# One layer of a hybrid decoder: lo parts of weights and diagonals of norms move from GpSimd to VectorE

## The chip, the cores and the metric

The kernel runs on one core of a Trainium2 chip. The metric is the device time of one execution in microseconds (us); the median of several runs counts. The engines are TensorE (PE in the profile, its weight loads PEld), VectorE (DVE), ScalarE (ACT), GpSimd (POOL) and SyncE (SP), which only issues transfers here.

## What is computed

The reference is one decoder layer on x of 512 rows and 1024 columns, in float32:

```python
h = rms_norm(x, attn_pre_g)
q_a, k_a, v_a, q_b, k_b, v_b = split(h @ w_in)
y_a = rms_norm(sliding_window_attention(q_a, k_a, v_a, sinks, alibi), swa_out_g)
y_b = rms_norm(softmax(q_b0 k_b0) v_b - lam * softmax(q_b1 k_b1) v_b, subln_g) * 0.8
x = x + rms_norm(concat(y_a, y_b) @ w_out, attn_post_g)
u = causal_dwconv3(rms_norm(x, ffn_pre_g) @ w_up)
x = x + rms_norm((gelu(u_g) * u_v) @ w_down, ffn_post_g)
```

`y_a` has 8 query heads over 2 key heads and a window of 128; `y_b` has 4 heads, each with two score maps of 64 columns and values of 128.

## The kernel before, in words

**Hi and lo parts.** Each matrix product runs in a reduced float32 format (F32R), with both operands split into a hi part (the value rounded to the format) and a lo part (the rest). A product is three matmuls: hi x hi, hi x lo, lo x hi. `load_split` (line 108) brings a weight of 128 x 1024 (or 128 x 960) in from memory over SP's queue (line 118), lets ScalarE copy it to hi (line 119), and lets VectorE or GpSimd subtract to give lo (line 120). Which of the two it is, the argument `slow` says. `raw` has two buffers for what comes in, and the pool of hi and lo tiles has three of each.

**The order of weights.** `Stream` (line 123) holds a list of loads and keeps two ahead of the one in use. The list (lines 153 to 161) has 29 loads: 6 for values, 10 for queries and keys, 13 for the output projection (8, then 5 once more). All are marked slow, and then `W_FIRST = 10` and `W_LAST = 10` take the mark off the first ten and the last ten. So nine splits run on GpSimd: those of the last six loads of queries and keys, and of the first three of the output projection. Later weights (up and down projection) always take VectorE.

**Norms.** `spread_a` (line 167) turns a row of sums of squares into a factor that is the same in all partitions. TensorE sums over partitions (line 174), VectorE adds epsilon (177 or 179), GpSimd takes the power -1/2 (181), VectorE splits the result into hi and lo columns (184, 185), and `eng` multiplies the identity by each column (190). The results are two diagonals of 128 x 128 for each block of 128 rows, up to 128 x 512 in one instruction. `spread_b` (196) multiplies them by ones on TensorE (200) and copies the result out on ScalarE (202). The call for the first norm (244) passes VectorE as `eng`; the six others (one at 619, five at 478) use the default, GpSimd: four of them make diagonals of 128 x 512, two of 128 x 256.

**The stages.** First the transposed x and the first keys and queries are handled (216 to 242). Then the sliding-window attention and the differential attention run as chains of small steps (`swa_a` to `swa_e`, `diff_a` to `diff_e`). Between these steps a queue of filler work for TensorE is drained: projections (356), values (276), the output projection (516). Each filler has a cost in us, and `fill(us)` (260) takes as many as the chain step leaves room for. After that come the row norms (642, 664), the up projection with convolution (698, 808), and the down projection with seven products in place of eight (885). The framework lays the instructions of each engine out in a fixed order when the kernel is built; an engine runs them in that order, and each waits for its inputs.

**Names and lines in the steps.** A finished projection is multiplied out of its bank by VectorE (351, `evac`). Keys are split by ScalarE (389) and VectorE (390) and copied to the other half of the partitions by transfers that GpSimd issues (391, 392). Queries are scaled and split by ScalarE (381) and VectorE (382); TensorE needs both for the scores (397, 398). VectorE takes the scores out with their minimum (425), ScalarE exponentiates (430), VectorE combines the two maps (434 to 436), TensorE transposes (452) and VectorE splits the transposed block (402). The window's output is scaled at 626, each head's at 484. GpSimd also fills masks (321 to 334), sums squares of x (239), and makes the row norms' roots (637 to 639).

Of the kernel before, what the change touches and what calls it, by code (L numbers as in the profile page):

```python
# [13 lines left out]
ALU = mybir.AluOpType  # L14
# [4 lines left out]
D = 1024  # L19
NT = S // P  # L20
NK = D // P
# [14 lines left out]
PAD = 72  # L36

WARM = 8

W_FIRST, W_LAST = 10, 10  # L40

V_AFTER = 1

# [16 lines left out]
def fl(t):  # L60
    return t.bitcast(F32)
# [16 lines left out]
def hymba_layer(ctx, tc, x, st, wv, wqk, w_out, w_up, w_down, conv, cols, lam_in, sinks, gpost, gffn, gfin, out):  # L78
    nc = tc.nc
    TT = nc.vector.tensor_tensor  # L80
# [24 lines left out]
    a8 = Arena(wk, T8, [P, NT, S], F32R, "a8")  # L105


    def load_split(src, slow=False, p=None, big=False, r=None):
        n = src.shape[-1]
        if r is None:  # L110
            r = raw.tile([P, n], F32, tag="raw", name="wr")
        if big:
            t = a8.get()
            h, l = (t[:, 2 * m:2 * m + 2].rearrange("p a s -> p (a s)") for m in range(2))
        else:
            t = None
            h, l = ((p or wsp).tile([P, n], F32R, tag=m, name=f"w{m}") for m in ("hi", "lo"))
        nc.sync.dma_start(r, src)
        ACT(h, r, AF.Copy)  # L119
        (nc.gpsimd if slow else nc.vector).tensor_tensor(l, r, fl(h), op=ALU.subtract)  # L120
        return (h, l, t) if big else (h, l)

    class Stream:
# [5 lines left out]
        def next(self):  # L129
            while len(self.made) < min(self.used + 1 + self.ahead, len(self.jobs)):  # L130
                src, kw = self.jobs[len(self.made)]
                self.made.append(load_split(src, **kw))
            self.used += 1
            return self.made[self.used - 1]
# [15 lines left out]
    ident = const.tile([P, P], F32, name="ident")  # L150
    make_identity(nc, ident)

    slow = dict(slow=True)
    jobs = []
    q = [(wqk[i], slow) for i in range(10)]
    o = [(w_out[k], slow) for k in range(NK)]
    v = [(wv[i], slow) for i in range(6)]
    nv = 2 + 2 * V_AFTER
    jobs += v[0:3] + q[0:nv] + v[3:6] + q[nv:10] + o + [(w, dict(big=True, **kw)) for w, kw in o[4::-1]]
    for n in [*range(W_FIRST), *range(len(jobs) - W_LAST, len(jobs))]:  # L160
        jobs[n] = jobs[n][0], {**jobs[n][1], "slow": False}
    W = Stream(jobs, 2)

    ones_r = const.tile([P, P], F32R, name="ones_r")
    nc.vector.tensor_copy(ones_r, ones)

    def spread_a(sq, ts_, n=None, eps=None, r=None, eng=nc.gpsimd):


        if r is None:  # L170
            r = small.tile([P, NT], F32, tag="rb", name="rb")
        o = banks.get()
        for t in ts_:
            nc.tensor.matmul(o[:, t:t + 1], lhsT=sq[:, t * P:(t + 1) * P], rhs=ones[:, 0:1], start=True, stop=True)
        c, cs = slice(ts_[0], ts_[-1] + 1), slice(ts_[0] * P, (ts_[-1] + 1) * P)
        if eps is None:
            nc.vector.tensor_scalar(r[:, c], o[:, c], 1.0 / n, EPS, op0=ALU.mult, op1=ALU.add)
        else:
            TT(r[:, c], o[:, c], eps[:, c], op=ALU.add)
        banks.free(o)  # L180
        nc.gpsimd.tensor_tensor(r[:, c], r[:, c], mhalf[:, c], op=ALU.pow)
        rh = small.tile([P, NT], F32R, tag="rh", name="rh")
        rl = small.tile([P, NT], F32, tag="rl", name="rl")
        nc.vector.tensor_copy(rh[:, c], r[:, c])
        TT(rl[:, c], r[:, c], fl(rh[:, c]), op=ALU.subtract)
        ds = []
        for part in (fl(rh), rl):
            d = t2()
            shape = [P, len(ts_), P]
            eng.tensor_tensor(  # L190
                d[:, cs].rearrange("p (t q) -> p t q", q=P), ident.unsqueeze(1).broadcast_to(shape),
                part[:, c].unsqueeze(2).broadcast_to(shape), op=ALU.mult)
            ds.append(d)
        return ds, cs

    def spread_b(ds, cs):

        o, rb = banks.get(), f2.get()
        for m, d in enumerate(ds):
            nc.tensor.matmul(o[:, cs], lhsT=ones_r, rhs=d[:, cs], start=(m == 0), stop=(m == 1))  # L200
        a2.free(*ds)
        ACT(rb[:, cs], o[:, cs], AF.Copy)
        banks.free(o)
        return rb
# [10 lines left out]
    xss = f2.get()  # L215
    for k in range(NK):
        r = a4.get()
# [8 lines left out]
        h, l = t2(), t2()  # L226
# [14 lines left out]
        a4.free(r)  # L241
        a2.free(h, l)
    rs1 = const.tile([P, NT], F32, name="rs1")
    rbc = spread_b(*spread_a(xss, range(NT), D, r=rs1, eng=nc.vector))
    f2.free(xss)


# [228 lines left out]
    def diff_d(h, ts_):  # L476
        pv, sq = soft[h]
        soft[h] = pv, sq, spread_a(sq, ts_, eps=zq[h])
# [139 lines left out]
    def swa_d():  # L618
        soft["a"] = spread_a(sqa[0], range(NT), 4 * P)
        f2.free(sqa[0])  # L620
# [14 lines left out]
    def sum_rstd(s2):  # L635

        nc.gpsimd.tensor_scalar(s2[:, 0:1], s2[:, 0:1], 1.0 / D, EPS, op0=ALU.mult, op1=ALU.add)  # L637
        nc.gpsimd.tensor_scalar(s2[:, 1:2], s2[:, 1:2], 1.0 / D, s2[:, 0:1], op0=ALU.mult, op1=ALU.add)
        nc.gpsimd.tensor_tensor(s2[:, 1:2], s2[:, 1:2], mhalf[:, 0:1], op=ALU.pow)  # L639
        return s2[:, 1:2]  # L640
# [54 lines left out]
    def early_weights(c):  # L695
        ew.append(load_split(w_up[order[c]], big=True)[0:2])
# [49 lines left out]
    for h, last in enumerate((3, 7, 11, 13)):  # L746
        n, ts_ = last + DEP + 1, range(NT) if h < 3 else range(2, 4)
# [4 lines left out]
    for n in range(2, len(steps) + DEP):  # L752
        if n < len(steps):
            h, i = steps[n]
# [80 lines left out]
    for n, f in enumerate(order):  # L835
# [4 lines left out]
        else:  # L840
            w = U.next()
# [3 lines left out]
        if n % 2:  # L845
            k = n // 2
# [42 lines left out]
    def prepare():  # L889
        p, q = steps_d[len(ready)]  # L890
        kind, src = products[p]
        src = w_down[q, src] if isinstance(src, int) else sums[src, q]

        n = len(ready)
        r = None if n % 3 == 0 else wsum.tile([P, D], F32, tag=f"b{n % 6 - n % 6 // 3 - 1}", name="wr")
        w = load_split(src, r=r, p=dw if n % 4 == 3 else None)
        a = rows(q, kind)
        ah = sp.tile([P, 2, S // 2], F32R, tag="ah", name="ah")
        al = sp.tile([P, 2, S // 2], F32R, tag="al", name="al")
        split(a, ah, al)  # L900
        ready.append((*w, ah, al))
# [93 lines left out]
    for s in two:  # L995
# [4 lines left out]
        r = sum_rstd(s2[s])  # L1000
# [59 lines left out]
```

## Time and profile before

| | before |
|---|---|
| median of 3 runs | 742.37 us (739.88 to 742.78) |
| the profiled execution: time | 741.13 us |
| its span, first to last instruction | 739.4 us |
| mean granted TensorE clock | 0.991 |
| TensorE busy | 717.2 us, 97% |
| VectorE busy | 557.2 us, 75% |
| ScalarE busy | 377.5 us, 51% |
| GpSimd busy | 108.8 us, 15% |

The busy shares are means over all stages. An engine's idle time counts only where another waits for it, and a row of the timeline ends with the idle time before it in brackets and what ended it. The granted clock is given as a share of 2.4 GHz: 1.00 is 2.4 GHz, 0.50 is 1.2 GHz. Letters before the colon of a tile name are the program's names; `a` is a tile of the attention's arenas, `bank` a PSUM bank.

### The profile page before, as it was taken

To read this page: it belongs to the slowest core of one execution; us is meant where nothing else is said; L and a number is where in the kernel's file an instruction comes from. 1 tells how busy PE (TensorE), PEld (TensorE's weight loads), DVE (VectorE), ACT (ScalarE), POOL (GpSimd) and SP (SyncE) were. 2 spreads that over 40 slices of the span, in tenths; PEclk is the share of its full clock that TensorE was granted. 3 is DMA by queue.
4 is the path that set the end of the run, shared out by engine and by line. 5 is a ranking of instruction groups with operands and counts; after the bars stand their busy time and mean duration, and the time that the engine had idled before them with its cause. 6 is when DMAs were issued, how large, how long until landed. Compare 5 with 4: busy or idle time off the path is not lost.

```text
span 739.4 us, 9503 instructions
## 1 busy us (share of the span) xinstructions
PE 717.2 (97%) x3416; PEld 599.3 (81%) x3416; DVE 557.2 (75%) x868; ACT 377.5 (51%) x652; POOL 108.8 (15%) x154
## 2 busy tenths in 40 slices
PE   8999998988999999999999999999999999999995
PEld 6787897767789988888888888888888888888884
DVE  7899968988779478685675757657566699988983
ACT  5288865756466334433434334333333666656661
POOL 6300145451333010000000000000000000000301
PEclk9999998999999999999999999999999999999999
DMA  7432314235455476555565555655576555556631
GB/s 226 148 101 69 88 59 114 57 86 170 116 170 172 171 257 241 186 204 195 170 207 190 203 185 198 204 181 200 175 252 215 160 193 199 199 187 189 205 131 58
DMA packets 36815, 124.43 MB, mean 168 GB/s; under 512 B 4512, under 2 KB 5152, under 8 KB 36768
## 3 DMA queue, kind: packets, MB, share of 16 engines
q1 hardware_dynamic: 30240, 103.38, 43.3%
q0 software_dynamic: 6528, 20.45, 7.8%
q8 instruction: 27, 0.44, 0.3%
q14 instruction: 20, 0.16, 0.1%
HBM read 102.31 MB, written 18.87 MB: 164 GB/s over the span
## 4 chain that ended last, share of the span: by engine, by line
PE 68%; DVE 0%; POOL 0%; ACT 0%; issue 0%; POOLq 0%; DVEq 0%; ACTq 0%
PE bank L703 16%; PE bank L702 16%; PE bank L704 16%; PE bank L907 7%; PE bank L909 7%; PE bank L908 7%; PE bank L668 0%; DVE f L1003 0%; POOL r L637 0%; DVE f L661 0%; DVE a L656 0%; ACT f L657 0%; ACT jk L944 0%; POOLq L1056 0%; POOL r L639 0%
## 5 line engine op out<-in xcount | busy, mean ns | idle before, releaser
L120 DVE TENSOR_TENSOR wlo<-wr,whi 128x1024 fp32r<-128x1024 f32 (+1 forms) x132 | 161.0, 1220 | 114.4 <-ACT whi L119 114.2
L119 ACT ACTIVATE whi<-wr 128x1024 fp32r<-128x1024 f32 (+1 forms) x141 | 149.0, 1057 | 166.1 <-PE bank L703 103.7
L702 PE MATMUL bank<-hTh,whi 128*128 128x512 f32 (+1 forms) x496 | 191.3, 386 | 0.0
L703 PE MATMUL bank<-hTl,whi 128*128 128x512 f32 (+1 forms) x496 | 191.3, 386 | 0.0
L704 PE MATMUL bank<-hTh,wlo 128*128 128x512 f32 (+1 forms) x496 | 191.2, 386 | 0.0
L702 PEld LDWEIGHTS bank<-hTh,whi 128*128 128x128 f32 x496 | 93.2, 188 | 18.8
L704 PEld LDWEIGHTS bank<-hTh,wlo 128*128 128x128 f32 x496 | 93.2, 188 | 18.6
L703 PEld LDWEIGHTS bank<-hTl,whi 128*128 128x128 f32 x496 | 93.2, 188 | 18.6
L908 PE MATMUL bank<-whi,al 128*128 128x512 f32 x224 | 87.1, 389 | 0.0
L909 PE MATMUL bank<-wlo,ah 128*128 128x512 f32 x224 | 87.1, 389 | 0.0
L907 PE MATMUL bank<-whi,ah 128*128 128x512 f32 x224 | 87.1, 389 | 0.0
L848 ACT ACTIVATE a<-ct 128x512 f32<-128x512 f32 x32 | 20.2, 631 | 90.3 <-DVE ct L813 90.3
L811 ACT ACTIVATE ct<-bank,conv_sb 128x512 f32<-128x512 f32 x64 | 48.6, 760 | 9.3 <-PE bank L704 9.3
L812 DVE SCALAR_TENSOR_TENSOR ct<-bank,conv_sb,ct 128x511 f32<-128x511 f32 x64 | 47.6, 744 | 7.7 <-ACT ct L811 7.7
L907 PEld LDWEIGHTS bank<-whi,ah 128*128 128x128 f32 x224 | 42.0, 188 | 8.9 <-ACT m L957 0.2
L909 PEld LDWEIGHTS bank<-wlo,ah 128*128 128x128 f32 x224 | 42.0, 188 | 8.8
L908 PEld LDWEIGHTS bank<-whi,al 128*128 128x128 f32 x224 | 42.0, 188 | 8.7
L813 DVE SCALAR_TENSOR_TENSOR ct<-bank,conv_sb,ct 128x510 f32<-128x510 f32 x64 | 47.7, 746 | 1.3
L827 DVE TENSOR_TENSOR b<-b,b 128x1024 f32<-128x1024 f32 x32 | 38.9, 1216 | 7.2 <-DMA b<-in_w_down 7.2
L402 DVE TENSOR_TENSOR al<-act,ah 128x512 fp32r<-128x512 f32 x48 | 32.8, 684 | 2.1 <-ACT ah L401 2.1
L401 ACT ACTIVATE ah<-act 128x512 fp32r<-128x512 f32 x48 | 29.5, 615 | 8.4 <-DVE act L849 5.6
L366 PE MATMUL bank<-hTh,whi 128*128 128x512 f32 x80 | 32.9, 411 | 0.0
(203 smaller groups left out, 1145.1 us busy)
## 6 DMA issues: line engine op xcount, KB each, us to landing
wr<-in_w_up SPq DMA_DIRECT2D x64, 512.0 KB, 3.6
b<-in_w_down SPq DMA_DIRECT2D x32, 512.0 KB, 4.5
wr<-in_w_down SPq DMA_DIRECT2D x24, 512.0 KB, 3.7
wr<-in_w_out SPq DMA_DIRECT2D x13, 512.0 KB, 4.3
wr<-in_wqk SPq DMA_DIRECT2D x10, 512.0 KB, 3.6
U<-b POOLq DMA_DIRECT2D x8, 512.0 KB, 3.7
W<-b POOLq DMA_DIRECT2D x8, 512.0 KB, 3.0
V<-b POOLq DMA_DIRECT2D x8, 512.0 KB, 3.0
```

Of the source, the lines that this page charges most:

```text
L119: ACT(h, r, AF.Copy)
L120: (nc.gpsimd if slow else nc.vector).tensor_tensor(l, r, fl(h), op=ALU.subtract)
L702: nc.tensor.matmul(u[:, c0:c1], lhsT=h[:, c], rhs=hTh[k][:, c0:c1], start=(k == 0), stop=False)
L703: nc.tensor.matmul(u[:, c0:c1], lhsT=h[:, c], rhs=hTl[k][:, c0:c1], start=False, stop=False)
L704: nc.tensor.matmul(u[:, c0:c1], lhsT=l[:, c], rhs=hTh[k][:, c0:c1], start=False, stop=(k == NK - 1))
L811: ACT(ct, u, AF.Identity, bias=w(3), scale=w(2))
L812: STT(ct[:, 1:S], u[:, 0:S - 1], w(1), ct[:, 1:S], ALU.mult, ALU.add)
L813: STT(ct[:, 2:S], u[:, 0:S - 2], w(0), ct[:, 2:S], ALU.mult, ALU.add)
L827: TT(rawb[a], rawb[a], rawb[b], op=ALU.add)
L907: nc.tensor.matmul(o, lhsT=ah[:, j, rs], rhs=wh[:, cs], start=first and j == 0, stop=False, skip_group_check=True)
L908: nc.tensor.matmul(o, lhsT=al[:, j, rs], rhs=wh[:, cs], start=False, stop=False, skip_group_check=True)
L909: nc.tensor.matmul(o, lhsT=ah[:, j, rs], rhs=wl[:, cs], start=False, stop=last and j == 1, skip_group_check=True)
```

## The change

All lo parts of weights are made by VectorE, and all diagonals of norms too. The lists of loads and their order, the calls of `spread_a` and the power at line 181 are as they were. GpSimd keeps that power, the masks, its transfers, the sums at line 239 and the row roots.

```diff
--- before.py
+++ after.py
@@ -37,8 +37,6 @@
 
 WARM = 8
 
-W_FIRST, W_LAST = 10, 10
-
 V_AFTER = 1
 
 NORM_ACT = 2
@@ -105,7 +103,7 @@
     a8 = Arena(wk, T8, [P, NT, S], F32R, "a8")
 
 
-    def load_split(src, slow=False, p=None, big=False, r=None):
+    def load_split(src, p=None, big=False, r=None):
         n = src.shape[-1]
         if r is None:
             r = raw.tile([P, n], F32, tag="raw", name="wr")
@@ -117,7 +115,7 @@
             h, l = ((p or wsp).tile([P, n], F32R, tag=m, name=f"w{m}") for m in ("hi", "lo"))
         nc.sync.dma_start(r, src)
         ACT(h, r, AF.Copy)
-        (nc.gpsimd if slow else nc.vector).tensor_tensor(l, r, fl(h), op=ALU.subtract)
+        TT(l, r, fl(h), op=ALU.subtract)
         return (h, l, t) if big else (h, l)
 
     class Stream:
@@ -150,21 +148,18 @@
     ident = const.tile([P, P], F32, name="ident")
     make_identity(nc, ident)
 
-    slow = dict(slow=True)
     jobs = []
-    q = [(wqk[i], slow) for i in range(10)]
-    o = [(w_out[k], slow) for k in range(NK)]
-    v = [(wv[i], slow) for i in range(6)]
+    q = [(wqk[i], {}) for i in range(10)]
+    o = [(w_out[k], {}) for k in range(NK)]
+    v = [(wv[i], {}) for i in range(6)]
     nv = 2 + 2 * V_AFTER
-    jobs += v[0:3] + q[0:nv] + v[3:6] + q[nv:10] + o + [(w, dict(big=True, **kw)) for w, kw in o[4::-1]]
-    for n in [*range(W_FIRST), *range(len(jobs) - W_LAST, len(jobs))]:
-        jobs[n] = jobs[n][0], {**jobs[n][1], "slow": False}
+    jobs += v[0:3] + q[0:nv] + v[3:6] + q[nv:10] + o + [(w, dict(big=True)) for w, kw in o[4::-1]]
     W = Stream(jobs, 2)
 
     ones_r = const.tile([P, P], F32R, name="ones_r")
     nc.vector.tensor_copy(ones_r, ones)
 
-    def spread_a(sq, ts_, n=None, eps=None, r=None, eng=nc.gpsimd):
+    def spread_a(sq, ts_, n=None, eps=None, r=None):
 
 
         if r is None:
@@ -187,7 +182,7 @@
         for part in (fl(rh), rl):
             d = t2()
             shape = [P, len(ts_), P]
-            eng.tensor_tensor(
+            TT(
                 d[:, cs].rearrange("p (t q) -> p t q", q=P), ident.unsqueeze(1).broadcast_to(shape),
                 part[:, c].unsqueeze(2).broadcast_to(shape), op=ALU.mult)
             ds.append(d)
@@ -241,7 +236,7 @@
         a4.free(r)
         a2.free(h, l)
     rs1 = const.tile([P, NT], F32, name="rs1")
-    rbc = spread_b(*spread_a(xss, range(NT), D, r=rs1, eng=nc.vector))
+    rbc = spread_b(*spread_a(xss, range(NT), D, r=rs1))
     f2.free(xss)
```

## Rows read from the trace of the kernel before

**Rows 1.** Stretches: us, busy by engine (instructions), PEclk, DMA share, GB/s.

```profile
100.00:110.00 10.00, 10.00 (x53) 8.81 (x53) 4.57 (x14) 6.50 (x12) 7.10 (x5) 1.00 0.34 106
110.00:175.00 65.00, 56.90 (x268) 45.65 (x268) 57.81 (x126) 40.60 (x97) 32.32 (x33) 0.95 0.34 88
175.00:205.00 30.00, 29.12 (x155) 24.07 (x155) 21.25 (x51) 16.87 (x39) 8.15 (x11) 1.00 0.54 164
```

**Rows 2.** Timeline of TensorE: start, us, what, idle before with its releaser.

```profile
122.04 0.48 PE L397 MATMUL bank<-a,a 128*128 128x256 f32 x1 [1.96 <-DVE a L382]
...
143.98 0.50 PE L200 MATMUL bank<-a,ones_r 128*128 128x512 f32 x1 [0.60 <-POOL a L190]
145.12 0.50 PE L200 MATMUL bank<-a,ones_r 128*128 128x512 f32 x1 [0.64 <-POOL a L190]
...
150.37 0.39 PE L397 MATMUL bank<-a,a 128*128 128x256 f32 x1 [2.02 <-DVE a L382]
...
170.31 0.44 PE L397 MATMUL bank<-a,a 128*128 128x384 f32 x1 [1.84 <-DVE a L382]
```

**Rows 3.** Single microseconds after the first of these waits, columns as before.

```profile
122.00:123.00 1.00, 0.96 (x4) 0.86 (x5) 0.96 (x2) 0.00 (x0) 0.00 (x0) 0.58 0.58 111
128.00:129.00 1.00, 1.00 (x4) 0.62 (x3) 0.96 (x3) 0.09 (x1) 0.90 (x2) 0.50 0.00 0
```

**Rows 4.** Timeline of GpSimd: three of the six splits from 110 to 175.

```profile
115.79 2.43 POOL L120 TENSOR_TENSOR wlo<-wr,whi 128x1024 fp32r<-128x1024 f32 x1
118.58 2.85 POOL L120 TENSOR_TENSOR wlo<-wr,whi 128x1024 fp32r<-128x1024 f32 x1 [0.36 <-ACT whi L119]
...
166.89 2.81 POOL L120 TENSOR_TENSOR wlo<-wr,whi 128x1024 fp32r<-128x1024 f32 x1
```

**Rows 5.** Timeline of VectorE.

```profile
119.24 3.45 DVE L382 SCALAR_TENSOR_TENSOR a<-f,a 64x512 fp32r<-64x512 f32 x2
...
129.85 0.48 DVE L436 SCALAR_TENSOR_TENSOR a<-a,zd 128x256 f32<-128x256 f32 x1
...
146.08 0.68 DVE L382 SCALAR_TENSOR_TENSOR a<-f,a 64x512 fp32r<-64x512 f32 x1
...
147.58 2.73 DVE L382 SCALAR_TENSOR_TENSOR a<-f,a 64x512 fp32r<-64x512 f32 x1
...
164.84 0.16 DVE L185 TENSOR_TENSOR rl<-rb,rh 128x4 f32<-128x4 f32 x1
...
167.51 3.46 DVE L382 SCALAR_TENSOR_TENSOR a<-f,a 64x512 fp32r<-64x512 f32 x2
...
171.82 1.22 DVE L120 TENSOR_TENSOR wlo<-wr,whi 128x1024 fp32r<-128x1024 f32 x1
172.95 0.75 DVE L484 SCALAR_TENSOR_TENSOR f<-bank,g_sub,f 128x512 f32<-128x512 f32 x1
```

**Rows 6.** Line 190, the diagonals: duration min/median/max in ns, first and last start.

```profile
L190 POOL TENSOR_TENSOR a<-ident,rh x6: 612/1040/1041, 127.1 to 203.4; 128x512 fp32r<-128x512 f32 x4, 128x256 fp32r<-128x256 f32 x2
...
L190 DVE TENSOR_TENSOR a<-ident,rh x1: 683/683/683, 31.3 to 31.3; 128x512 fp32r<-128x512 f32 x1
```

**Rows 7.** Groups of VectorE by form, 100 to 205 us: busy, mean ns, idle before.

```profile
L382 DVE SCALAR_TENSOR_TENSOR a<-f,a 64x512 fp32r<-64x512 f32 x6 | 10.3, 1712 | 0.2
...
L626 DVE SCALAR_TENSOR_TENSOR a<-a,cols_sb,f 128x512 f32<-128x512 f32 x4 | 4.6, 1188 | 0.0
...
L436 DVE SCALAR_TENSOR_TENSOR a<-a,zd 128x256 f32<-128x256 f32 x4 | 3.8, 945 | 0.1
...
L185 DVE TENSOR_TENSOR rl<-rb,rh 128x4 f32<-128x4 f32 x4 | 2.2, 561 | 0.0
```

**Rows 8.** Groups of GpSimd: the splits.

```profile
L120 POOL TENSOR_TENSOR wlo<-wr,whi 128x1024 fp32r<-128x1024 f32 x9 | 22.7, 2527 | 19.0 <-ACT whi L119 18.9
```

**Rows 9.** Line 120 up to 100 us: what VectorE waited for before its splits.

```profile
  ACT whi L119: 2.0, 3
```

**Rows 10.** A stretch with two splits on VectorE, columns as in rows 1.

```profile
45.00:50.00 5.00, 4.98 (x30) 4.24 (x30) 4.91 (x15) 5.00 (x14) 0.00 (x0) 1.00 0.36 107
```

## The prediction

> **What bounds the kernel now.** I read the stretches first, then TensorE's idle time in them, then what ended each wait. Nine lo splits and six pairs of diagonals are all that moves, and they lie between 100 and 205 us; so that stretch is cut in three [rows 1]. Outside it the change touches no instruction. From 100 to 110 TensorE is never idle and VectorE is busy for 4.57 of 10 us. From 110 to 175 TensorE is busy for 56.90 of 65 us at a granted clock of 0.95, and VectorE for 57.81: it is the fuller engine here. From 175 to 205 TensorE loses under 1 us. What can be won or lost is therefore in the middle 65 us: 8.1 us of idle TensorE, and 5% of clock.
>
> The larger waits of that idle time are five [rows 2]. Three are for L382 (the lo rows of a query) and last 1.96, 2.02 and 1.84 us; two, 0.60 and 0.64 us, are for the diagonals that GpSimd makes at L190. Right after the first the granted clock is low: 0.58 in the microsecond from 122, 0.50 in the one from 128 [rows 3], 1.2 instead of 2.4 GHz. About 7 us at half clock lose some 3.4 us, and 5% of 65 us is 3.3: so this is the one such stretch in the 65 us, and the waits of 2.02 and 1.84 us were followed by none.
>
> Why is L382 late? Six splits run on GpSimd in the 65 us; the first, second and last start at 115.79, 118.58 and 166.89 [rows 4]. The second ends at 121.43. VectorE's pair of L382 starts at 119.24 and takes 3.45 us, where one of them alone takes 0.68 [rows 5]: it ends 1.26 us after GpSimd's split. The pair at 167.51 takes 3.46 and ends 1.27 us after the last split. So an instruction of VectorE with two inputs in SBUF stands still while GpSimd's tensor_tensor runs. It is no share of bandwidth, since the rest of each pair takes its usual time.
>
> **The change, part by part.** *Added to VectorE:* a split of 128x1024 takes 1.22 us, and the next instruction starts 1.13 us after it [rows 5]; nine are 10.2. A full diagonal takes 0.68 us there, against 1.04 on GpSimd [rows 6]; the twelve are eight full ones and four of half width (0.4 each, an estimate from the ratio of GpSimd's two, 0.61 to 1.04): 5.4 + 1.6 = 7.0. Together 17.2 us. Inside the 65 us it is six splits and three pairs of full diagonals: 6.8 + 4.1 = 10.9.
>
> *Taken from VectorE:* the blocked time. By groups from 100 to 205 [rows 7]: L382 10.3 less 6 x 0.68 = 6.2; L626 4.6 less 4 x 0.75 (the 0.75 is L484's, of the same size [rows 5]) = 1.6; L436 of 256 columns 3.8 less 4 x 0.48 = 1.9; L185 2.2 less 4 x 0.16 = 1.6. That is 11.3 us, a floor, since L436's other lengths are left out. L382, L626 and by their starts half of the other two lie inside the 65 us: 6.2 + 1.6 + 1.8 = 9.6. So VectorE's load there goes from 57.8 to 57.8 - 9.6 + 10.9 = 59.1 us, hardly more, though it does 10.9 us more work.
>
> *Taken from GpSimd:* 22.7 us of splits [rows 8] and all diagonals. Nobody waits for those splits (each is needed two weights later), so this gains nothing itself. Its copies of keys (L391, L392) are queued behind splits and come earlier; I put that at nothing, because no TensorE wait of rows 2 is for them. It keeps the power at L181, the masks, the sums at L239 and the row roots of L637 to L639. The hop from VectorE to GpSimd and back for the power stays. The raw buffers come free 1.3 us sooner per split (2.5 against 1.22); the next loads start earlier on SP's queue, whose order does not change, and a later stage with those loads on time gains nothing.
>
> *A new wait:* a split at the head of VectorE's queue waits for its hi copy on ScalarE. Queued behind it are the evictions of scores (L425) and the next L382, for which TensorE waits. The ten splits that VectorE makes before 100 us cost 2.0 us of such waiting in 3 cases [rows 9]: between 0 and 0.67 us each. I take 0, since the order is laid out by readiness (at 119.24 both L382 were ahead of any other work), and keep 0.67 for the range.
>
> *The first three splits* (100 to 110 and at the edge) are hidden by VectorE's 5.4 idle us there; without that cover they would cost 3.4 us.
>
> Now wait by wait. **First (1.96):** two splits (2.26) come ahead of the pair, whose block (3.45 - 1.36 = 2.09) goes: +0.2 if both are ahead, -0.9 if the second falls behind the pair; I take -0.4. **The half clock** after it: 0 to -3.4. A wait cut from 2.0 to 1.6 need not end it, but two waits of this length left the clock at full, so I take it as gone; VectorE, with a pair of diagonals more there, cannot follow all of it: -2.5. **The diagonals (0.60 + 0.64):** each is 0.36 shorter on VectorE, -0.7 if nothing goes between, 0 if something does; -0.4. **Second L382 (2.02):** its block (2.73 - 0.68 = 2.05) goes, a pair of diagonals (1.36) comes ahead: -0.7 with the split behind, +0.4 with it ahead; -0.6, since the split started on GpSimd when this L382 was next. **Third (1.84):** block 3.46 - 1.36 = 2.1 against the same 1.36 and 1.13: -0.7 to +0.4; -0.5. After 175: nothing, because VectorE is idle for 9 of 30 us there.
>
> Sum: -0.4 - 2.5 - 0.4 - 0.6 - 0.5 = -4.4 us. Ends: +1.0 (all splits ahead, the clock unchanged) and -6.4. A check by load: VectorE can be 98% busy with TensorE full, as from 45 to 50 us, with splits of its own among its work (4.91 and 4.98 of 5) [rows 10]. 59.1 / 0.98 = 60.3 us, so the 65 us cannot shrink by more than 4.7, and the sum just fits under that.
>
> The profiled execution took 741.13 us (span 739.40 and 1.73 around it), 1.24 under the median of the three runs, 742.37; on it the sum gives 736.7, on the median 738.0, which I forecast.
>
> One rule speaks against the change. The trace shows VectorE at 89% of the 65 us, the fuller engine [rows 1]. The Trainium skill (Perfetto Trace Analysis, Optimizing Scalar/DVE Operations) says that work may be offloaded from a saturated VectorE, even to GpSimd, and adds that the two share a read port, so that it might not help. By its first half the change goes the wrong way (rival 3 prices that); by its second half, with which the blocked pairs of rows 5 agree, it is near neutral in load, as in my sum.
>
> **The rivals.** *1. The half clock stays,* or comes after another wait. For it: the first wait shrinks by little. Against it: two waits of like length left the clock alone. Time: 742.4 - 1.9 = 740.5.
>
> *2. A new order takes the gain back.* The splits are placed ahead of the pairs each time: the upper ends, +0.2, +0.4 and +0.4, and the clock unchanged: 743.4 at worst, 742.4 as the middle. For it: a split needs only one copy of 1 us and may be ready first. Against it: the L382 are issued earlier in the program.
>
> *3. VectorE becomes the bound (slower).* The place is the same 65 us: the 10.9 us come in full, and the blocked time turns out to be slack that VectorE spends waiting for TensorE or ScalarE instead. Nothing shed: (57.8 + 10.9) / 0.98 = 70.1, +5.1, 747.5 us; with 0.67 us of wait at each of six splits, +9.1, 751.5. It decides from the point where VectorE sheds under 5 of the 9.6 us: then its load passes 63.7, and 63.7 / 0.98 is 65. Against it: all three long waits end on a blocked L382, so the blocked time is on the path.
>
> *4. Everything goes.* TensorE gets most of the 8.1 idle us and the clock back, about -8, 734. It needs VectorE fuller than rows 10 show, or a blocked time well over my floor.
>
> That the change does less than it says I rule out: every split passes through the one function, and every diagonal through L190.
>
> **How the numbers follow.** Forecast 0.48 (its own range 735.5 to 740), rival 1 0.22, rival 2 0.12, rival 3 0.13, rival 4 0.05. The range 734 to 745.5 takes in the forecast, rivals 1, 2 and 4 and the near edge of 3. A measurement of this kernel tells about 0.5% (3.7 us) from no change, so faster means under 738.7 and slower over 746.1. Faster: three quarters of the forecast, rival 4 and a little of rival 1, 0.45. Slower: rival 3 and the tail of 2, 0.16. The same: 0.39.
>
> **What would show it.** In the changed profile: L382 at 0.7 us in every instance, L626 at 0.75; no tensor_tensor of more than 1.1 us on GpSimd between 100 and 205; VectorE's load in the 65 us near 59; the granted clock 1.00 after 120 us; the three waits for L382 together under 4.5 us. I am wrong if L382 stays long, if VectorE waits for hi copies over 4 us in that stretch, or if new waits of TensorE for L425 or L402 appear.

## The result, and the profile after

The changed kernel took 731.99 us (median of 4 runs, 731.16 to 732.63), the kernel before 741.25 us (4 runs, 739.88 to 742.78): a ratio of 0.9878 [0.986, 0.9896], so 9.3 us less, where 4.4 were forecast. Its profiled execution took 731.16 us, with a span of 729.4 and a mean granted clock of 0.997. VectorE is now busy for 558.2 us in all (557.2 before), GpSimd for 74.5 (108.8). In the changed file line numbers up to `load_split` are smaller by 2, later ones by 5: L382 is L377, L120 is L118, L190 is L185.

Windows of the changed kernel (busy us of TensorE, weight loads, VectorE, ScalarE, GpSimd, with counts; then clock, DMA share, GB/s), to be held against [rows 1, 3]:

```profile
100.00:110.00 10.00, 10.00 (x53) 8.71 (x52) 7.95 (x18) 6.24 (x14) 0.61 (x3) 1.00 0.45 130
110.00:175.00 65.00, 62.42 (x315) 51.21 (x314) 60.32 (x154) 44.77 (x106) 10.04 (x19) 1.00 0.38 110
175.00:205.00 30.00, 29.65 (x153) 23.91 (x152) 24.98 (x51) 18.94 (x46) 7.75 (x14) 1.00 0.48 146
...
122.00:123.00 1.00, 1.00 (x9) 0.92 (x9) 0.60 (x4) 0.19 (x1) 0.00 (x0) 1.00 0.56 217
...
128.00:129.00 1.00, 1.00 (x6) 0.81 (x5) 1.00 (x3) 0.52 (x1) 0.00 (x0) 1.00 0.00 0
```

The 65 us are not the same work in the two kernels, since the changed one gets further in them (315 matmuls, 268 before). The same work (but for a few matmuls that the new order moves over the edge), up to the same score matmuls, is one window of each. Before, then after:

```profile
110.00:174.80 64.80, 56.70 (x267) 45.47 (x267) 57.61 (x126) 40.40 (x97) 32.32 (x33) 0.95 0.34 87
```

```profile
109.60:166.30 56.70, 54.12 (x273) 44.11 (x272) 52.94 (x134) 39.50 (x94) 10.04 (x19) 1.00 0.35 94
```

The stretch is 8.1 us shorter, the half clock is gone, and VectorE is busy for less time, though it has the splits and diagonals on top.

The waits of TensorE from 25 to 205 us (us in all, times, longest), after, hold none for the lo rows of queries any more:

```profile
PE bank L361 <- DVE f L479: 1.2, 1, 1.2
PE bank L195 <- DVE a L185: 0.5, 1, 0.5
PE bank L392 <- DVE m L542: 0.4, 1, 0.4
...
PE bank L447 <- DVE md L420: 0.3, 1, 0.3
```

VectorE's groups by form, 100 to 205 us, after (count, busy us, mean ns), against [rows 7]:

```profile
L118 DVE TENSOR_TENSOR wlo<-wr,whi 128x1024 fp32r<-128x1024 f32 x14 | 17.1, 1221 | 2.3 <-ACT whi L117 2.1
...
L377 DVE SCALAR_TENSOR_TENSOR a<-f,a 64x512 fp32r<-64x512 f32 x6 | 4.1, 686 | 0.2
...
L621 DVE SCALAR_TENSOR_TENSOR a<-a,cols_sb,f 128x512 f32<-128x512 f32 x4 | 2.8, 744 | 0.0
L185 DVE TENSOR_TENSOR a<-ident,rh 128x512 fp32r<-128x512 f32 x4 | 2.7, 685 | 0.0
...
L431 DVE SCALAR_TENSOR_TENSOR a<-a,zd 128x256 f32<-128x256 f32 x4 | 1.9, 475 | 0.0
...
L180 DVE TENSOR_TENSOR rl<-rb,rh 128x4 f32<-128x4 f32 x4 | 0.6, 154 | 0.0
```

Six L377 take 686 ns each instead of 1712, four L621 take 744 instead of 1188: every instruction of VectorE from 100 to 205 us is back within 0.1 us of the shortest length of its form. And VectorE's timeline at the place of the first wait, after:

```profile
119.42 1.22 DVE L118 TENSOR_TENSOR wlo<-wr,whi 128x1024 fp32r<-128x1024 f32 x1
120.67 1.40 DVE L377 SCALAR_TENSOR_TENSOR a<-f,a 64x512 fp32r<-64x512 f32 x2
```

Before, the pair started at 119.24 and took 3.45 [rows 5]. Here a split stands right ahead of it, it starts later, and it still ends 0.6 us sooner. TensorE does not wait for it, and its own order is one reason: the score that stood right behind the L366 at 119.69, and waited there [rows 2], has other matmuls ahead of it now, 15 from 119.52 to 122.04:

```profile
119.30 0.39 PE L361 MATMUL bank<-hTh,whi 128*128 128x512 f32 x1
119.52 0.39 PE L362 MATMUL bank<-hTl,whi 128*128 128x512 f32 x1
...
122.04 0.28 PE L392 MATMUL bank<-a,a 128*128 128x256 f32 x1
```

The gain by landmarks, as TensorE starts the same matmul in both: at the last value product (L290) 0.4 us (103.12 to 102.73), at the first L467 5.0 (133.34 to 128.33), at the last score (L397) 8.7 (186.92 to 178.21), at the first L668 9.8 (218.81 to 208.97). So 4.6 us come from 103 to 133, 3.7 from 133 to 187, 1.1 behind that.

### The profile page after: what moved, and what is told of

Same layout as the page of the kernel before. It is cut to its first block, busy times and chain, and to the rows that moved or that the text cites. A ratio compares the mean times of both kernels' runs of the same rounds, so it can differ in the third digit from the quotient of the medians.

```text
span 729.4 us, 9488 instructions
## 1 busy us (share of the span) xinstructions
PE 711.9 (98%) x3416; PEld 595.0 (82%) x3416; DVE 558.2 (77%) x889; ACT 377.2 (52%) x652; POOL 74.5 (10%) x133
## 4 chain that ended last, share of the span: by engine, by line
PE 69%; DVE 0%; POOL 0%; ACT 0%; issue 0%; POOLq 0%; DVEq 0%; ACTq 0%
PE bank L698 16%; PE bank L697 16%; PE bank L699 16%; PE bank L902 7%; PE bank L903 7%; PE bank L904 7%; PE bank L663 0%; DVE f L998 0%; POOL r L632 0%; DVE f L656 0%; DVE a L651 0%; ACT f L652 0%; ACT jk L939 0%; POOLq L1051 0%; POOL r L634 0%
## 5 line engine op out<-in xcount | busy, mean ns | idle before, releaser
L118 DVE TENSOR_TENSOR wlo<-wr,whi 128x1024 fp32r<-128x1024 f32 (+1 forms) x141 | 172.0, 1220 | 113.3 <-ACT whi L117 112.8
L397 DVE TENSOR_TENSOR al<-act,ah 128x512 fp32r<-128x512 f32 x48 | 32.8, 684 | 2.1 <-ACT ah L396 2.1
```

The costliest lines, as they stand in the source:

```text
L118: TT(l, r, fl(h), op=ALU.subtract)
```

## The experiments

The question was why twice the forecast. **Theory** (L in the expectations): VectorE stands still while GpSimd reads SBUF; that time returns in full, and most of the work added to VectorE falls into its idle time. **Rivals:** GpSimd's lateness or its load was the cause, whatever it does (G); the new order of instructions is the gain (O); the added work counts one for one and something else gained. A "ghost" is an extra GpSimd instruction whose result nobody reads. All kernels with their times, sorted by what makes the splits and diagonals, each ratio to the kernel before measured beside it (741.25 us beside the changed kernel, 740.2 to 740.3 beside the others). In the edits, `...` stands for lines left out, such as those that mark the nine splits:

| run | nine splits | diagonals | beside it | us | ratio |
|---|---|---|---|---|---|
| after | VectorE | VectorE | | 731.99 | 0.9878 [0.986, 0.9896] |
| e1_splits | VectorE | GpSimd | | 734.33 | 0.9918 [0.9903, 0.9933] |
| e2_diags | GpSimd | VectorE | | 737.57 | 0.9958 [0.9943, 0.9973] |
| e3_ghost | VectorE | VectorE | GpSimd reads | 738.95 | 0.9975 [0.9962, 0.9989] |
| e4_ghostw | VectorE | VectorE | GpSimd writes | 733.06 | 0.9902 [0.9885, 0.9918] |
| e8_ghostall | VectorE | VectorE | GpSimd reads more | 748.9 | 1.0119 [1.0092, 1.0147] |
| e5_pieces | GpSimd, in quarters | GpSimd | | 735.72 | 0.9936 [0.9917, 0.9954] |
| e9_fill | left out | GpSimd | GpSimd writes | 730.9 | 0.9865 [0.9842, 0.9888] |
| e11_skip | left out | VectorE | GpSimd writes | 729.05 | 0.9839 [0.9821, 0.9857] |
| e10_twice | VectorE, twice | VectorE | | 741.66 | 1.0016 [1.0006, 1.0026] |
| e6_xss | VectorE | VectorE | sums too on VectorE | 725.76 | 0.9805 [0.9784, 0.9827] |

**Either half alone.** The splits alone:

```diff
-W_FIRST, W_LAST = 10, 10
+W_FIRST, W_LAST = 10, 19
```

> The nine splits go to VectorE, the diagonals stay on GpSimd. Theory L (VectorE stands still while a GpSimd instruction reads SBUF): in the trace of before, 9.3 of the 13.1 us of blocked time between 100 and 205 us stand beside splits, 3.8 beside diagonals; so about 70% of the change's 9.3 us, 734 to 736 us. Theory G (GpSimd's results come late): no one waited for a split, so 741 us, as before. Theory O (the new fixed order of TensorE's work is what helps): this kernel's order differs from both, so anything between 731 and 742.

The diagonals alone:

```diff
-            eng.tensor_tensor(
+            nc.vector.tensor_tensor(
```

> The twelve diagonals go to VectorE, the nine splits stay on GpSimd. Theory L: the smaller share of the blocked time goes (3.8 of 13.1) and the three late L382 stay, so 738 to 741 us. Theory G: the only waits of TensorE for GpSimd (1.7 us at the diagonals) go, and nothing else is to be had, so 739 to 740, and all of that comes from here. The half clock after 122 us stays by L.

The splits give 0.0082 and the diagonals 0.0042, together 0.0124 beside the 0.0122 of both: within their intervals the halves add. e2_diags came out 0.4 us under the 738 to 741 expected; the late L382 that it was to keep are two and not three. What each leaves behind is in TensorE's waits from 25 to 205 us. With GpSimd's diagonals left (e1_splits) it is those; with its splits left (e2_diags) it is L382, and the half clock with it (0.83 from 120 to 140 us), and once, for 2.45 us, the diagonals that VectorE makes now:

```profile
PE bank L200 <- POOL a L190: 2.7, 5, 0.9
```

```profile
PE bank L397 <- DVE a L382: 2.7, 2, 2.0
PE bank L200 <- DVE a L190: 2.5, 1, 2.5
```

**Is it GpSimd's reading?** The changed kernel, with nine additions on GpSimd (hi plus the identity) into a tile that nobody reads. Then the same place with GpSimd only writing (two memsets), but for a copy of one column:

```diff
...
+            nc.gpsimd.tensor_tensor(scratch.rearrange("p (t q) -> p t q", q=P), fl(h).rearrange("p (t q) -> p t q", q=P),
+                                    ident.unsqueeze(1).broadcast_to([P, 8, P]), op=ALU.add)
...
```

> The changed kernel, and at each of the nine splits GpSimd also adds the hi part and the identity into a tile that nobody reads: an instruction of the split's size that reads SBUF, with no result that anyone waits for. The order of TensorE, VectorE and ScalarE is that of the changed kernel, line by line. Theory L: the blocking comes back without the dependence: 736 to 741 us, and single instructions of VectorE at L377, L431 or L621 two to three times as long. Theories G and O: 731 to 733, as the changed kernel.

```diff
...
+            nc.gpsimd.tensor_copy(scratch[:, 0:1], fl(h)[:, 0:1])
+            for _ in range(2):
+                nc.gpsimd.memset(scratch, 0.0)
...
```

> As the one with the extra additions, but at each of the nine splits GpSimd fills that tile twice with zeros instead (after a copy of one column that ties it to the hi part): GpSimd is busy for about as long, and writes SBUF but hardly reads it. Theory L in its narrow form (reads collide): 731 to 733 us, as the changed kernel. If any busy GpSimd slows VectorE, by its write port or otherwise: as with the additions, 736 to 741.

The additions cost 7 us (738.95 against 731.99), though nobody waits for them and the fixed order of TensorE, VectorE and ScalarE is that of the changed kernel. The timeline of e3_ghost shows the block where it had been: the two start together and VectorE's split takes 3.44 instead of 1.22 us; 2.54 us of waiting follow on TensorE, for the lo rows (here L383):

```profile
120.71 2.38 POOL L120 TENSOR_TENSOR scratch<-whi,ident 128x1024 f32<-128x1024 f32 x1 [1.08 <-ACT whi L117]
...
120.74 3.44 DVE L118 TENSOR_TENSOR wlo<-wr,whi 128x1024 fp32r<-128x1024 f32 x1
...
124.95 0.39 PE L398 MATMUL bank<-a,a 128*128 128x256 f32 x1 [2.54 <-DVE a L383]
```

With writes (e4_ghostw) GpSimd works for 17.2 us, where the splits took 22.7 [rows 8], and VectorE's L384 (the lo rows) and L628 stay at 686 and 746 ns. The time, 733.06, is at the edge of the 731 to 733 expected; its interval and that of the changed kernel overlap, so the 1.1 us between the medians are not told from nothing:

```profile
L122 POOL MEMSET scratch<- 128x1024 f32 x18 | 17.2, 955 | 1.0
```

```profile
L384 DVE SCALAR_TENSOR_TENSOR a<-f,a 64x512 fp32r<-64x512 f32 x6 | 4.1, 686 | 0.2
...
L628 DVE SCALAR_TENSOR_TENSOR a<-a,cols_sb,f 128x512 f32<-128x512 f32 x4 | 2.8, 746 | 0.0
```

**The same order, less of a block.** In the kernel before, each split on GpSimd is cut in four; the order of every engine stays as it was, but for the pieces:

```diff
-        (nc.gpsimd if slow else nc.vector).tensor_tensor(l, r, fl(h), op=ALU.subtract)
...
+            for c in range(0, n, n // 4):
+                cs = slice(c, c + n // 4)
+                nc.gpsimd.tensor_tensor(l[:, cs], r[:, cs], fl(h)[:, cs], op=ALU.subtract)
...
```

> The kernel before, each of GpSimd's nine splits cut into four of 256 columns: the same engine, the same data, the same order on TensorE and VectorE line by line, but no single GpSimd instruction lasts over about 0.7 us. Theory L, if VectorE gets in between two pieces: a blocked instruction loses at most 0.7 instead of 2 us, so the nine splits' 9.3 us of blocked time fall to about a third and 736 to 738.5 us come out. If it only gets in when GpSimd has nothing more to do: 740 to 741, as before. Theory G (GpSimd's lateness): four instructions take no less time than one, so 740 to 742.

4.5 us faster than before (0.3 us under the 736 to 738.5 expected), with more work on GpSimd: the splits' group below is 30.2 us, 22.7 before [rows 8]. In its timeline the pair of L387 (the lo rows) slips in between pieces and takes 2.25 us instead of 3.45 [rows 5]; the wait of 1.96 [rows 2] is 0.34, and no half clock follows:

```profile
115.90 6.98 POOL L123 TENSOR_TENSOR wlo<-wr,whi 128x256 fp32r<-128x256 f32 x8
...
119.35 2.25 DVE L387 SCALAR_TENSOR_TENSOR a<-f,a 64x512 fp32r<-64x512 f32 x2
...
120.52 0.39 PE L402 MATMUL bank<-a,a 128*128 128x256 f32 x1 [0.34 <-DVE a L387]
```

```profile
L123 POOL TENSOR_TENSOR wlo<-wr,whi 128x256 fp32r<-128x256 f32 x36 | 30.2, 869 | 13.8 <-ACT whi L119 13.8
```

So it is neither GpSimd's load nor its lateness.

**What the block was worth, with nothing added.** In the kernel before, GpSimd subtracts two columns and then fills the lo tile instead of subtracting it all, in the old order; beside it, a fill in the changed kernel, and that kernel with each of the nine splits made twice on VectorE:

```diff
-        (nc.gpsimd if slow else nc.vector).tensor_tensor(l, r, fl(h), op=ALU.subtract)
...
+            nc.gpsimd.tensor_tensor(l[:, 0:2], r[:, 0:2], fl(h)[:, 0:2], op=ALU.subtract)
+            for _ in range(2):
+                nc.gpsimd.memset(fl(l), 0.0)
...
```

> The kernel before, with its nine GpSimd splits replaced: GpSimd subtracts two columns and then fills the lo part with zeros twice, so the lo parts of these nine weights are left out of the result. The order of TensorE, VectorE and ScalarE is that of the kernel before, line by line; VectorE gets no added work, and GpSimd hardly reads SBUF. It prices two things against the run with only the splits moved (0.9918 of before): the ten us of splits on VectorE, and the new order. Theory L with added work and order for nothing: 0.990 to 0.993, 733 to 735 us. If the added work costs TensorE something: below 0.988. If the old order itself costs (TensorE waits for L382 where the new order gives it other work first): above 0.994.

```diff
-        TT(l, r, fl(h), op=ALU.subtract)
+        nc.gpsimd.memset(fl(l), 0.0) if skip else TT(l, r, fl(h), op=ALU.subtract)
...
```

> The changed kernel with the subtraction of the nine moved splits left out and the lo tile filled with zeros by one GpSimd memset, so the lo parts of these nine weights are left out of the result. VectorE has 11 us less work between 100 and 205 us than in the changed kernel, and nothing blocks it. Theory (the added work lay in slack): 730 to 732.5 us, within 2 us of the changed kernel. Rival (one for one): 721 to 725 us.

```diff
-        TT(l, r, fl(h), op=ALU.subtract)
+        [TT(l, r, fl(h), op=ALU.subtract) for _ in range(2 if twice else 1)]
...
```

> The changed kernel with each of the nine moved splits made twice on VectorE (the same subtraction into the same tile): 9 x 1.22 = 11 us more work on VectorE between 100 and 205 us, six of them, 7.3 us, between 110 and 175. GpSimd is as in the changed kernel. Theory (added work on VectorE is free as long as VectorE has idle time): VectorE is idle for 4.7 of those 65 us after the change, so the first splits cost nothing and what lies beyond the slack is paid: 733 to 737 us against 732 for the changed kernel. Rival (what the prediction did: added work counts one for one against the path there): 7.3 to 11 us more, 739 to 743 us. In both, L377 stays at 0.69 us.

Without the block, and with the order as before, 9.4 us go (e9_fill, 730.9). VectorE's pair runs at its full rate beside a GpSimd that is writing:

```profile
120.24 1.41 DVE L387 SCALAR_TENSOR_TENSOR a<-f,a 64x512 fp32r<-64x512 f32 x2
...
120.32 1.97 POOL L123 MEMSET wlo<- 128x1024 f32 x2
```

So the splits' block alone is worth as much as the whole change, in the old order. The 733 to 735 expected, with added work and new order for nothing, were missed: against e1_splits, where VectorE makes the same nine splits, e9_fill is 0.0053 or 3.9 us faster, the price of the added splits and of their order together.

That price comes by dose. From no split on VectorE (e11_skip) to one each (the changed kernel), 11 us of VectorE's work between 100 and 205 us cost 0.0039, or 2.9 us (the two intervals lie just apart). From one to two (e10_twice), the next 11 us cost 0.0138, or 10.2 us. Each dose has an order of its own, though: matmul by matmul, TensorE's order differs from that of the changed kernel at 154 places of 3416 in e11_skip and at 257 in e10_twice. So these are prices of the work with the order that the framework lays out for it. The expectation of 733 to 737 for the second dose fell, and its rival's number held; that for e11_skip missed by 1 us. The windows 110 to 175 us of e11_skip, then of e10_twice, show how full VectorE is (after stands between them, with 60.32):

```profile
110.00:175.00 65.00, 64.24 (x330) 53.16 (x328) 57.15 (x156) 47.45 (x114) 16.00 (x26) 1.00 0.38 114
```

```profile
110.00:175.00 65.00, 58.48 (x280) 46.66 (x279) 61.28 (x146) 40.14 (x94) 10.05 (x19) 0.97 0.29 78
```

In e11_skip VectorE still has 7.9 us idle; in the changed kernel 4.7; in e10_twice 3.7, and yet the kernel gets less done (280 matmuls, 315 after). That VectorE can be filled no further there is an argument and was not tested; the new order may have its share. There TensorE waits for it, for L377 again and for the score evictions, although no instruction is lengthened (L377 687 ns, L118 1220):

```profile
PE bank L392 <- DVE a L377: 2.1, 1, 2.1
PE bank L361 <- DVE md L420: 1.6, 1, 1.6
```

**More reads.** The changed kernel with the nine additions of e3_ghost, and a GpSimd multiplication of a diagonal's size behind each of the twelve diagonals:

```diff
...
+                nc.gpsimd.tensor_tensor(
+                    scratch[:, cs].rearrange("p (t q) -> p t q", q=P), ident.unsqueeze(1).broadcast_to(shape),
+                    part[:, c].unsqueeze(2).broadcast_to(shape), op=ALU.mult)
...
```

> The changed kernel with extra GpSimd instructions whose results nobody reads, for both kinds of work: the nine additions of the earlier run, and one multiplication of a diagonal's size beside each of the twelve diagonals. The orders of the three engines are those of the changed kernel. Theory L: all of the blocking is back, 739 to 742 us, as before the change, though no result comes from GpSimd. If the new order or the shorter path of the diagonals carried a part of the gain, that part stays: below 739.

It took 748.9 us, over every expectation. The multiplications meet the very diagonals that TensorE waits for: VectorE's lo diagonals, in the group below, take 1811 ns instead of 684.

```profile
L191 DVE TENSOR_TENSOR a<-ident,rl 128x512 fp32r<-128x512 f32 x4 | 7.2, 1811 | 0.0
```

So the same work on both engines is worse than on either.

**A further place.** GpSimd still adds up squares while VectorE prepares the transposed x. The changed kernel with those sums on VectorE too:

```diff
-            nc.gpsimd.tensor_tensor(xss, xss, xsq, op=ALU.add)
+            TT(xss, xss, xsq, op=ALU.add)
```

> The changed kernel, and the seven sums of squares at the start (line 239 of the kernel before, 1.4 to 1.6 us each on GpSimd) made by VectorE as well. Theory L: VectorE's casts and subtractions of 0.4 to 0.75 us that last 1.4 to 1.8 between 8 and 24 us come back to their length (some 8 us), for seven additions of about 0.65 us; TensorE waits there for VectorE's lo rows (3.0 us), so 1 to 3 us faster than the changed kernel: 729 to 731. If that stretch is bound by the loads of x instead: 732, the same.

725.76 us (725.4 to 726.46), the fastest of all, 2% under the kernel before. The gain over the changed kernel is 6.2 us by the medians (5.4 by the ratios) where 1 to 3 were expected. VectorE's groups from 8 to 26 us, in the changed kernel and then here:

```profile
L220 DVE SCALAR_TENSOR_TENSOR hTl<-a,cols_sb,hTh 128x512 fp32r<-128x512 f32 x7 | 9.4, 1350 | 0.0
L223 DVE TENSOR_TENSOR a<-a,a 128x384 fp32r<-128x384 f32 x7 | 5.4, 772 | 0.1
L222 DVE CAST a<-a 128x384 fp32r<-128x384 f32 x7 | 5.1, 724 | 1.6 <-DMA a<-in_st 1.6
```

```profile
L220 DVE SCALAR_TENSOR_TENSOR hTl<-a,cols_sb,hTh 128x512 fp32r<-128x512 f32 x7 | 5.2, 743 | 0.0
L234 DVE TENSOR_TENSOR f<-f,f 128x512 f32<-128x512 f32 x7 | 4.8, 682 | 0.0
L223 DVE TENSOR_TENSOR a<-a,a 128x384 fp32r<-128x384 f32 x7 | 3.9, 551 | 0.0
L222 DVE CAST a<-a 128x384 fp32r<-128x384 f32 x6 | 2.1, 351 | 0.0
```

The first value product starts at 24.09 instead of 29.73 us: nearly the whole gain is made here. By these groups VectorE saves 8.3 us of lengthened instructions (one cast lies outside the second window) for 4.8 added; that GpSimd's masks also run earlier may be the rest, which was not tested.

**The kernel before, again.**

> The kernel before once more, for a second profile of it: is the half clock after 122 us there each time? If it belongs to the wait of 2 us ahead of it, it is there again at the same place; if it falls by chance, the wait is there and the clock stays at 1.00, or falls after another one of the three waits.

741.63 us in one run, with the five waits at 1.96, 0.65, 0.64, 2.02 and 1.84 us and the half clock at the same place. The waits belong to the kernel. The half clock is in both profiles, but not in every execution, as the next section shows.

## Why the prediction was right and wrong

**Right:** the place, the mechanism, and the sign. All that was to be seen in the changed profile is there: L377 at 684 to 689 ns in all 16 instances, L621 near 0.75 us, no tensor_tensor over 1.1 us on GpSimd, the clock at 1.00, the L382 waits gone (under 4.5 us was said). Of the signs of being wrong one is there, and small: a new wait of 0.3 us for the score evictions (L425 before, L420 now). Splits wait for hi copies for 2.1 us between 100 and 205 us, under the 4 that were set as the limit. Having GpSimd write instead of read removes the block (e4_ghostw, e9_fill); cutting its instruction shortens it (e5_pieces). The Trainium skill (SBUF — State Buffer, Who interferes with whom) says that a VectorE instruction with two SBUF inputs contends with a GpSimd instruction that reads SBUF, and not with one that only writes it. The traces of e3_ghost (3.44 us) and e4_ghostw (746 ns) agree.

**Wrong:** the size, 9.3 us instead of 4.4, under the range. The failed step is "now wait by wait", in which the work added to VectorE was charged against each wait. Taken gross, the step's own terms were about right: blocks of 2.09, 2.05 and 2.1 us and some 3.3 us of half clock are 9.5 us, and e9_fill, which takes away the splits' block and adds nothing, measured 9.4 (its interval goes from 8.3 to 11.7). That they come so close is in part luck, since the half clock is worth less (below). The charge was the error. With the 1.24 us of diagonal waits the gross is 10.8, the sum was 4.4, so 6.4 us were charged. Measured, the splits cost 2.9 (e11_skip to after), of which one part is seen on the path: in the changed kernel a split (145.47) stands right ahead of L479, and TensorE waits 1.2 us for L479; and moving the diagonals cost nothing on balance but won 3.1 (e2_diags), where I had put 1.36 for a pair of them ahead of each late L382.

Where did the charge go? For VectorE the step was right at the first wait: both splits (114.82 and 119.42) do come ahead of the pair, which starts 1.4 us later than before (120.67, 119.24) though its block is gone. What the step held fast was TensorE's order. The framework laid that out anew, and the scores that had waited stand 13 to 15 matmuls later in it at all three places, behind other work that was ready. In the old order TensorE would have been free for the first of them at 119.7 (119.30 and 0.39) and waited until about 121.4, when the first L377 of the pair ends (an estimate from 120.67 and 0.69): nearly as long as before. So added work that comes with other work for TensorE to do meanwhile is not charged. This is read from the trace; the changed kernel in the old order was not run, and how much of the difference belongs to the order stays open.

**The half clock's own share.** e9_fill has TensorE's order of the kernel before, so the same matmuls can be held side by side: from the score behind the first wait to the first L366 at full clock again, it is 7.28 us before (122.04 to 129.32) and 4.41 in e9_fill (120.98 to 125.39). So it cost 2.9 us in the profiled execution, not 3.3. And it is not in all: of the 44 executions of the kernel before beside the experiments, 12 have a mean granted clock of 0.996. By that mean 6 us of the whole execution are at half clock (twice 0.4% of 738), fewer than the 7 behind this wait. They took 739.9 us in the median; the 7 at 0.991, the mean of the profiled one, took 741.8. So some 2 us hang on it from one execution to another, and 7.9 us of the gain are there without it.

**The check by load,** which seemed to confirm the sum (59.1 us, at most -4.7), failed with it. It let VectorE shed only the floor, 9.6 us. Over the same work VectorE's load went from 57.6 to 52.9 us, 93% of the stretch; with the added 10.9 that is 15.6 shed. The block in that stretch, as the excess of each instruction over the shortest of its form, is 11.4 us before (L382 6.2, L436 2.5, L626 1.8, L185 0.9) and nothing after; the other 4.2 must be work that the new order does outside this stretch. So the load in the 65 us, near 59 as forecast (60.32), is right for the wrong reason: it holds more of the kernel.

**After 175 us** I had nothing; 1.1 us came behind the last score. With GpSimd's diagonals left (e1_splits) the kernel is a microsecond ahead of the changed one at its last score (177.12) and 3.2 behind at the first L668 (212.16). Of TensorE's waits between, 1.1 us are for those diagonals, 1.1 for VectorE's splits (L120) and 0.7 for L402, against 0.3 us of waits in the changed kernel; so lateness of the diagonals is a part of it, and the rest was not separated.

**The rivals.** 1 did not happen: the half clock went. Of 2, the condition came true at the first and the third place (the splits stand ahead of the pairs at 120.67 and 162.92), and its price did not, since TensorE's order moved too. Rival 3 (VectorE becomes the bound) did not happen at this dose, but e10_twice shows that its price is real: the next 11 us cost 10.2. The changed kernel is near that edge. What the prediction quoted from the Trainium skill (Perfetto Trace Analysis, Optimizing Scalar/DVE Operations), that a saturated VectorE may be offloaded even to GpSimd, does not hold here for work that reads SBUF: a VectorE at 89% is relieved by taking such work from GpSimd. The reservation beside it, that the shared port may spoil it, does hold. Rival 4 (everything goes, 734), to which I gave 0.05, was the nearest, with 2 us more. Its two conditions were asked of VectorE's load; of the second, more blocked time than the floor, 1.8 us were there (11.4 instead of 9.6).

**Still open:** how the part of the 6.4 us that did not come due divides between the new order of TensorE and the idle time of VectorE.

## What to carry to other kernels

Where a VectorE instruction with two inputs in SBUF shows two lengths, look for a GpSimd instruction over the long ones: the excess on the path comes back, here nearly one for one, by moving the GpSimd work or letting it only write, and in part by cutting it in pieces. Do not price the work that moves onto the engine wait by wait in the old order: the order is laid out anew, and the first 11 us cost 2.9 here, the next 11 cost 10.2. Idle time of the engine tells which way it goes and not the price: by it e10_twice was to take 737 us at most, and it took 741.66. A load that includes standing still is no measure of how full an engine is.

## What was unexpected of the hardware

A cast with one input is held up too. In the changed kernel's timeline of VectorE and GpSimd it takes 0.36 us alone and 1.46 beside GpSimd's sum, and ends 0.2 us after it:

```profile
7.67 0.36 DVE L222 CAST a<-a 128x384 fp32r<-128x384 f32 x1 [1.62 <-DMA a<-in_st]
...
9.00 1.45 POOL L234 TENSOR_TENSOR f<-f,f 128x512 f32<-128x512 f32 x1 [5.93 <-ACT f L233]
9.21 1.46 DVE L222 CAST a<-a 128x384 fp32r<-128x384 f32 x1
```

The half clock follows some waits and not others. A wait of 1.96 to 2.54 us that ends between 122 and 125 us was followed by 1.2 GHz in both profiles of the kernel before, in e2_diags and in e3_ghost; in e8_ghostall the clock fell already within the wait, at 124.0. In e2_diags the wait of 2.45 us at 146 us was followed by it too, and in e10_twice the wait of 2.06 us for L377 at 150 us, with no block near it. In e8_ghostall it came again at 154.7 us, 1.9 us after a wait of 1.42. Waits of 2.02 and 1.84 us in the kernel before and of 2.02 us in e8_ghostall (at 175 us) were not followed by it. What tells them apart no run here shows. In e10_twice:

```profile
150.00:151.00 1.00, 0.74 (x3) 0.75 (x4) 0.94 (x3) 0.42 (x1) 0.00 (x0) 0.63 0.00 0
151.00:152.00 1.00, 1.00 (x7) 1.00 (x6) 1.00 (x1) 0.00 (x0) 0.00 (x0) 0.50 0.00 0
```

The block goes both ways. In e5_pieces a quarter of a split takes 0.73 to 0.75 us on GpSimd, more than a quarter of the shortest whole one (2.39), and in 12 of the 36 cases 0.95 to 1.20 us. In each of these 12 a VectorE instruction with two inputs in SBUF (L387, L395, L441 or L631) runs beside it; VectorE instructions that read a PSUM bank do not lengthen it:

```profile
L123 POOL TENSOR_TENSOR wlo<-wr,whi x36: 729/742/1202, 101.1 to 165.2; 128x256 fp32r<-128x256 f32 x36
```
